# Another order of work in the head of a hybrid decoder layer, earlier loads at the start of its scan, and more buffers for the loads of v

## The chip, the cores and the metric

The kernel runs on one core of a Trainium2 chip. The metric is the device time of one execution in microseconds. Each kernel is run several times, and the median is compared.

## The reference

One layer on 1024 tokens of width 1024, behind 16 learned meta tokens (1040 rows), in float32:

```python
xn = rms_norm(h, mix_pre_g[l])
proj = xn @ w_in[l]                       # z, x, B, C, dt, q, k, v
...
y_ssd = ssd_mixer(z, xbc, dt_raw, ...)    # 2 groups, 16 heads of 64, state 128, chunks of 128
y_sb = rms_norm(stick_breaking_attention(q, k, v).reshape(Bsz, L, SB_WIDTH), sb_norm_g[l])
mix = jnp.concatenate([y_ssd, y_sb], axis=-1) @ w_out[l]
h = h + rms_norm(mix, mix_post_g[l])
xn = rms_norm(h, ffn_pre_g[l])
gu = xn @ w_up[l]
g = causal_dwconv(gu[..., :D_FF], ffn_conv_w[l], ffn_conv_b[l])
f = (jax.nn.gelu(g, approximate=True) * gu[..., D_FF:]) @ w_down[l]
h = h + rms_norm(f, ffn_post_g[l])
```

The mixer convolves x, B and C over four tokens, applies silu, takes dt through a softplus and runs a state space scan by chunks. The attention multiplies q and k of a head, turns the logits z into products of (1 - sigmoid) over the keys between query and key (a running product along the keys), and multiplies the weights with v.

## The kernel before, in words

Five engines work from queues of their own, each in the order of its instructions: TensorE (PE), VectorE (DVE), ScalarE (ACT), GpSimd (POOL), and SyncE (SP), which issues the DMAs. An instruction that waits holds up all that stands behind it on its engine; an instruction order for each engine follows from the order in which the program's text runs, with Python generators that interleave the stages.

A float32 operand of a matmul is split into a high part in a rounded format (fp32r) and a low part, the rest; a product is three matmuls, high by high, high by low, low by high. The high part is a copy on ScalarE, the low part a subtraction on VectorE or GpSimd. Large projections use products of sums of quarters of the operands (t1 to t4 are such sums of x, s24 and others such sums of weights), so that there are fewer products.

**Head** (L325 to L470, L579 to L602). Nine tiles of tokens, the meta tokens first, are loaded (`load_x`, L328), squared and summed by ScalarE (`square`, L354, tile junk), turned into 1/rms by GpSimd (`root`, L361, tiles ms and rs), multiplied by VectorE (`norm`, L365, tile xn) and transposed by TensorE (`turn_x`, L374, tile xtp, eight transposes a tile). A turn is read off by ScalarE (high parts, raw sums) and VectorE (low parts, sums). The weights of B and C of group 0 and of dt come in between (wr_B, wr_C, wr_dt); `split_hi` (L412) and `split_lo` (L418) split them. Their projections are chains of matmuls (`plain_steps`, L208, tiles pj_B and pj_C; `dt_steps`, L242, tile pj_dt): each of four pieces of 260 columns takes 24 matmuls for B and C, which may be cut in two half-chains of 12, and 16 for dt. The pieces go in the order QH: columns 0, then both of the second half of tokens, then 260. ScalarE copies B and C out of PSUM (craw, L236), VectorE dt (tile sq, L249). An explicit sequence at L424 to L463 says when each tile is squared, normed and turned and when a half-chain stands between two turns.

**Duos** (class `Duo`, L258): pairs of 128 columns of the projections of x, z, the other B and C, q and k, seven products each (dA, dX, dY of duo x or z, L308). GpSimd makes the low parts of their weights (wlo, L182) and the sums of weights (L285 to L288), VectorE adds the results (L320). The first duo, d0, begins behind the head. While duos run, the convolutions and transposes of the ones before are done between products.

**v** (L690 to L885). Seven products in the order VORDER, each in two halves s of four tiles t (`v_product`, L801); sums of quarters of the weights are made by `v_sums` (L854; tile vq, L791), and their splits by `v_split` (vwhi L727, vwlo L728). `v_out` stores v on SyncE's queue.

**Scan** (L990 to L1215). Units of a group and a chunk, prepared by `load_bc` (rows sl and sg that build the decay matrix), `load_state` (B, C of the group) and `load_x`; TensorE makes sg (L1059) as the first step of a unit. The projections of the q and k that are left go between the units as fill (`run(fill, n)`, six matmuls each), `put_stores` (L914) issues the stores of the fill that wait.

**Attention** (L1218 to L1480). Eight pairs of heads, eight blocks of queries each. For a block TensorE multiplies k and q (z, L1293), ScalarE takes the sigmoid of it (kp, L1294), VectorE the running product (kp, L1299), TensorE transposes the weights (tw, L1317) and multiplies them with v (av). `load_q` (L961) loads a block's q ahead (four tiles), `load_k` (L952) a pair's k. `load_v` (L1221) loads a pair's v in two versions, v (tile rv, two buffers) and w (tile rw, one buffer, in two pieces of five tiles and four), and GpSimd subtracts the second from the first (L1234). All these loads are issued by SyncE, in the order in which the generators run.

Then come the output projection (mo), the norms, the projections of the feed-forward layer (fA to fY) and the last one (dnA, dnB), where TensorE hardly waits.

## Time and profile before

| | us |
|---|---|
| median of 3 runs | 1688.15 (1682.5 to 1688.64) |
| the profiled execution | 1682.9 |
| its span | 1681.1 |
| TensorE busy in the span | 1635.2 |
| head and first duos | 0 to about 92 |
| v projection | about 350 to 431 |
| start of the scan | 431 to 450 |
| attention | 588 to 870 |

The profile is one execution; its times start at the span's start. Busy times are sums over an engine's instructions. PE is TensorE's matrix work, PEld its loads of weights. A wait names the instruction that waited and the one that ended the wait. The granted clock (PEclk) is the share of full speed that TensorE was given.

### The profile page before, as it was taken

To read this page: it belongs to the slowest core of one execution; us is meant where nothing else is said; L and a number is where in the kernel's file an instruction comes from. 1 tells how busy PE (TensorE), PEld (TensorE's weight loads), DVE (VectorE), ACT (ScalarE), POOL (GpSimd) and SP (SyncE) were. 2 spreads that over 40 slices of the span, in tenths; PEclk is the share of its full clock that TensorE was granted. 3 is DMA by queue.
4 is the path that set the end of the run, shared out by engine and by line. 5 is a ranking of instruction groups with operands and counts; after the bars stand their busy time and mean duration, and the time that the engine had idled before them with its cause. 6 is when DMAs were issued, how large, how long until landed. Compare 5 with 4: busy or idle time off the path is not lost.

```text
span 1681.1 us, 28980 instructions
## 1 busy us (share of the span) xinstructions
PE 1635.2 (97%) x11508; PEld 1442.2 (86%) x11508; DVE 1092.0 (65%) x1250; ACT 746.6 (44%) x1096; POOL 779.8 (46%) x583
## 2 busy tenths in 40 slices
PE   6899999999999999999999999999999999999998
PEld 5899999977877788888877889999998899888886
DVE  7776644345367689988841567666566666658777
ACT  6444344332244367766653245433333333344544
POOL 3576877520366454355332112777777776300001
PEclk9999999999999999999999999999999999999999
DMA  5443335333577875444345542332222333395335
GB/s 189 151 144 116 125 126 183 133 138 140 148 223 238 248 220 177 137 137 124 116 132 172 181 163 94 108 101 94 94 95 95 99 114 101 123 330 183 98 118 178
DMA packets 164518, 247.39 MB, mean 147 GB/s; under 512 B 18487, under 2 KB 99495, under 8 KB 162702
## 3 DMA queue, kind: packets, MB, share of 16 engines
q1 hardware_dynamic: 164382, 245.53, 45.0%
q8 instruction: 91, 1.49, 0.4%
q14 instruction: 45, 0.37, 0.1%
HBM read 161.99 MB, written 83.46 MB: 146 GB/s over the span
## 4 chain that ended last, share of the span: by engine, by line
PE 53%; DMA 0%; POOL 0%; ACT 0%; SPq 0%; issue 0%; DVE 0%; DVEq 0%; POOLq 0%; ACTq 0%
PE fX L1885 10%; PE mo L1489 9%; PE dnA L2297 7%; PE fY L1885 7%; PE fA L1885 7%; PE dnB L2297 5%; PE av L1337 2%; PE tw L1317 1%; PE z L1293 1%; PE g0a L1899 1%; DMA q<-qkd 0%; PE x2tp L1763 0%; PE g0d L1899 0%; PE g0c L1899 0%; PE u0a L1899 0%; PE u0d L1899 0%
## 5 line engine op out<-in xcount | busy, mean ns | idle before, releaser
L1299 DVE TENSOR_TENSOR_SCAN kp<-kp,hold 128x396 f32<-128x396 f32 (+5 forms) x224 | 211.5, 1015 | 30.6 <-ACT kp L1294 28.7
L182 POOL TENSOR_TENSOR wlo<-wr,whi 128x1024 fp32r<-128x1024 f32 x43 | 99.3, 2319 | 41.0 <-ACT whi L181 41.0
L2334 POOL TENSOR_TENSOR fms<-fms 128x1 f32<-128x1 f32 x8 | 2.3, 288 | 222.0 <-DMA ar<-fda 185.9
L181 ACT ACTIVATE whi<-wr 128x1024 fp32r<-128x1024 f32 x43 | 45.7, 1063 | 112.2 <-PE fX L1885 70.8
L1957 DVE SCALAR_TENSOR_TENSOR ga<-gr,pp,ga 128x1024 f32<-128x1024 f32 x44 | 69.3, 1574 | 34.0 <-ACT ga L1950 33.2
L2219 ACT ACTIVATE dh<-ar 128x512 fp32r<-128x512 f32 x77 | 48.6, 631 | 94.5 <-PE dnB L2297 44.7
L1294 ACT ACTIVATE kp<-z 128x788 f32<-128x788 f32 (+4 forms) x96 | 73.0, 833 | 26.5 <-PE z L1293 18.4
L2220 DVE TENSOR_TENSOR dl<-ar,dh 128x512 fp32r<-128x512 f32 x77 | 53.2, 691 | 47.0 <-ACT dh L2219 47.0
L1322 ACT ACTIVATE th<-tw 128x1024 f32<-128x1024 f32 (+2 forms) x96 | 70.8, 813 | 15.5 <-PE tw L1317 15.5
L1293 PE MATMUL z<-k,q 64*128 64x396 f32 (+9 forms) x672 | 65.2, 339 | 10.7 <-DMA q<-qkd 9.7
L1293 PEld LDWEIGHTS z<-k,q 64*128 64x128 f32 x672 | 56.5, 192 | 20.1 <-issue 11.0
L1317 PE MATMUL tw<-ident,kp 128*128 128x128 f32 x576 | 70.0, 276 | 0.8 <-ACT st L926 0.4
L1337 PE MATMUL av<-th,v 128*64 128x128 f32 x1152 | 70.0, 276 | 0.5 <-PE z L1293 0.5
L1317 PEld LDWEIGHTS tw<-ident,kp 128*128 128x128 f32 x576 | 62.4, 141 | 8.0 <-issue 7.2
L2297 PE MATMUL dnA<-dl,dh 128*128 128x512 f32 x176 | 68.5, 389 | 0.0
L2297 PE MATMUL dnA<-dh 128*128 128x512 f32 x176 | 68.5, 389 | 0.0
L2297 PE MATMUL dnA<-dh,dl 128*128 128x512 f32 x176 | 68.5, 389 | 0.0
L1337 PEld LDWEIGHTS av<-th,v 128*64 128x64 f32 x1152 | 62.3, 137 | 6.8 <-issue 4.8
L1271 POOL TENSOR_SCALAR cb<-kp 128x32 f32<-128x32 f32 x64 | 39.9, 632 | 56.4 <-DVE kp L1299 45.2
L2018 POOL TENSOR_TENSOR al<-wr,ah 128x512 fp32r<-128x512 f32 x20 | 28.6, 1428 | 77.6 <-ACT ah L2017 77.5
L2297 PE MATMUL dnB<-dh,dl 128*128 128x512 f32 x132 | 51.4, 389 | 0.0
L2297 PE MATMUL dnB<-dh 128*128 128x512 f32 x132 | 51.4, 389 | 0.0
(987 smaller groups left out, 6042.3 us busy)
## 6 DMA issues: line engine op xcount, KB each, us to landing
wr<-in_w_up SPq DMA_DIRECT2D x44, 512.0 KB
fds<-ga SPq DMA_DIRECT2D x44, 256.0 KB
b<-in_w_down SPq DMA_DIRECT2D x44, 256.0 KB
ar<-fds SPq DMA_DIRECT2D x44, 256.0 KB
fda<-ga SPq DMA_DIRECT2D x33, 256.0 KB
ar<-fda SPq DMA_DIRECT2D x33, 256.0 KB
k<-qkd SPq DMA_DIRECT2D x8, 1040.0 KB
q<-qkd SPq DMA_DIRECT2D x64, 128.0 KB
```

What stands on the lines that cost most here:

```text
L182: nc.gpsimd.tensor_tensor(l, raw, h.bitcast(F32), op=ALU.subtract)
L1293: mm(z[:, j, a - lo:e - lo], u[h, :], r[h, a - bases[x]:e - bases[x]], start=s_ == 0, stop=s_ == 2)
L1294: nc.scalar.activation(kp[:, :, lo:top], z[:, :, :top - lo], AF.Sigmoid, scale=-QSCALE)
L1299: nc.vector.tensor_tensor_scan(part, part, hold[:, L - last + a:L - last + e][:, ::-1], 1.0 if e == last else kp[:, j, e:e + 1], op0=ALU.m ...
L1317: nc.tensor.transpose(tw[:, j, b, :], kp[:, j, c0:c0 + P], ident)
L1322: copied[0] = nc.scalar.activation(th[:, :, :nb, :], tw[:, :, :nb, :], AF.Copy, scale=-1.0, bias=1.0).ins
L1337: mm(av[halves[j], 1 - x, :], v[:, kb, halves[j]], th[:, j, b, :], start=kb == 0, stop=kb == i)
L1489: recent[0] = mm(acc, u[:, k, :], v[:, cs], start=(k == 0 and j == 0), stop=(k == 7 and j == 2))
L1885: mm(acc[:, c, :nn], u[:, k, :], v[:, k, c0:c0 + nn], start=first and k == 0 and j == 0, stop=k == 3 and j == 2, skip_group_check=not first)
L1957: nc.vector.scalar_tensor_tensor(v, self.g[jj][:, :, i:i + 256], fconv_w[:, j, i:i + 1], v, op0=ALU.mult, op1=ALU.add)
L2220: sub(lo[:, k], raw, hi[:, k].bitcast(F32), op=ALU.subtract)
L2297: mm(banks[BANK[n], t], u[:, 0, c], v[:, 1, :], start=(n in (1, 2, 5) and p == 0 and i == 0), stop=(p == NPR - 1 and i == 2), skip_group_c ...
```

## The change

In the head, the load of wr_B goes ahead of gpre (the norm's gain), that of wr_dt gets a buffer of its own and goes behind x3, and that of wr_C goes behind x5. The low parts of B and C are each one subtraction on VectorE instead of two halves on GpSimd. dt is copied out by ScalarE. The pieces of B, C and dt go in the order QC (columns 0 and 260 of the first half of tokens, then of the second), and half-chains or whole chains stand between the turns from the fourth tile on. Behind the head, the splits of the first duo's weights come in another order, and its third split ahead of that of t2.

In the v projection, the tail and the sums of weights for the product behind come one product step earlier, the first split of product 6 too, and the last four stores of v are issued by ScalarE. At the start of the scan, twelve fills stand ahead of the first unit instead of eight, the rows of each of the three buffers are set on their own, and the loads of the second unit are issued behind four fills, ahead of `put_stores`. In the attention, v has three buffers and w two.

```diff
-SCAN_FILL, FIRST = 39, 8
+SCAN_FILL, FIRST = 39, 12
...
-        return raw, plain_steps(w, ev, nm, halves_)
+        return raw, plain_steps(w, ev, nm, halves_, 0, QC)
...
-        for half, c in QH:
+        for half, c in QC:
...
-            nc.vector.tensor_copy(dtT[:, half * TH + c:half * TH + c + CQ], acc[:32, :CQ])
+            nc.scalar.activation(dtT[:, half * TH + c:half * TH + c + CQ], acc[:32, :CQ], AF.Copy)
...
         load_x(0)
         load_x(1)
+        raws = {"B0": raw_of("B0", w_xbc[8])}
         gpre = row_bcast(pre, 0, D, "gpre")
         load_x(2)
         load_x(3)
+        raw_dt = pre.tile([P, KB, 16], F32, tag="wdt", name="wr_dt", bufs=1)
+        nc.sync.dma_start(out=raw_dt, in_=w_dt)
         load_x(4)
-        raw_dt = wp.tile([P, KB, 16], F32, tag="wraw", name="wr_dt")
-        nc.sync.dma_start(out=raw_dt, in_=w_dt)
-        raws = {"B0": raw_of("B0", w_xbc[8])}
-        for i in range(5, NT):
+        load_x(5)
+        raws["C0"] = raw_of("C0", w_xbc[10])
+        for i in range(6, NT + 1):
             load_x(i)
-        raws["C0"] = raw_of("C0", w_xbc[10])
-        load_x(NT)
         nc.sync.dma_start(out=pp, in_=parts)
...
-        def split_lo(name, part):
-            ks = slice(4 * part, 4 * part + 4)
-            nc.gpsimd.tensor_tensor(ws[name][1][:, ks], raws[name][:, ks], ws[name][0][:, ks].bitcast(F32),
-                                    op=ALU.subtract)
-
-        chains = []
-        for i in range(3):
+        def split_lo(name):
+            nc.vector.tensor_tensor(ws[name][1], raws[name], ws[name][0].bitcast(F32), op=ALU.subtract)
+
+        for i in range(2):
             square(i)
             root(i)
         norm(0)
         norm(1)
-        for i in range(NT + 1):
-            if i == 4:
-                run(dt_chain, 1)
-            if i not in (2, 3):
-                norm(i + 2)
-            turn_x(i)
-            if i != 2:
-                square(i + 2 if i == 3 else i + 3)
-                root(i + 2 if i == 3 else i + 3)
-            if i == 3:
-                norm(4)
-                norm(5)
-            if i == 1:
-                hl = tq.tile([P, KB, 32], F32R, tag="wdt", name="wh_dt")
-                nc.scalar.activation(hl[:, :, 0:16], raw_dt, AF.Copy)
-                nc.gpsimd.tensor_tensor(hl[:, :, 16:32], raw_dt, hl[:, :, 0:16].bitcast(F32), op=ALU.subtract)
-                dt_chain = dt_steps(hl)
-            if i in (3, 4):
-                split_hi("B0" if i == 3 else "C0")
-            if i in (3, 4, 5):
-                split_lo("B0" if i < 4 else "C0", int(i == 5))
-            if i == 3:
-                square(6)
-                root(6)
-                split_lo("B0", 1)
-            if i == 3:
-                chains.append(conv_chain("B0", ws["B0"]))
-            if i == 5:
-                raw_x0 = [raw_of(f"x0{j}", w_xbc[j]) for j in range(2)]
-            if i in (5, 6):
-                run(chains[0][1], 1)
-            if i == 6:
-                chains.append(conv_chain("C0", ws["C0"]))
-            if i in (7, 8):
-                run(chains[1][1], 1)
+        split_hi("B0")
+        split_lo("B0")
+        square(2)
+        root(2)
+        norm(2)
+        turn_x(0)
+        square(3)
+        root(3)
+        norm(3)
+        turn_x(1)
+        hl = tq.tile([P, KB, 32], F32R, tag="wdt", name="wh_dt")
+        nc.scalar.activation(hl[:, :, 0:16], raw_dt, AF.Copy)
+        nc.gpsimd.tensor_tensor(hl[:, :, 16:32], raw_dt, hl[:, :, 0:16].bitcast(F32), op=ALU.subtract)
+        dt_chain = dt_steps(hl)
+        chains = [conv_chain("B0", ws["B0"])]
+        square(4)
+        root(4)
+        turn_x(2)
+        norm(4)
+        square(5)
+        root(5)
+        turn_x(3)
+        norm(5)
+        run(dt_chain, 1)
+        split_hi("C0")
+        split_lo("C0")
+        chains.append(conv_chain("C0", ws["C0"]))
+        run(chains[0][1], 1)
+        turn_x(4)
+        square(6)
+        root(6)
+        norm(6)
+        run(chains[0][1], 1)
+        run(chains[1][1], 1)
+        turn_x(5)
+        square(7)
+        root(7)
+        norm(7)
+        run(chains[1][1], 1)
+        run(dt_chain, 1)
+        turn_x(6)
+        square(8)
+        root(8)
+        norm(8)
+        raw_x0 = [raw_of(f"x0{j}", w_xbc[j]) for j in range(2)]
+        run(chains[0][1], 2)
+        turn_x(7)
+        run(chains[1][1], 2)
+        turn_x(8)
...
     d0 = duos[0]
     d0.r = raw_x0
+    d0.split_22()
     run(dt_chain, 1)
-    run(chains[0][1], 2)
-    d0.split_22()
+    run(chains[0][1], 1)
+    d0.split_1()
     split_t(t1r, xo["t1"], nc.vector)
+    run(chains[0][1], 1)
+    d0.sums()
     run(chains[1][1], 2)
     for act in late:
         act()
-    d0.split_1()
-    run(chains[0][1], 2)
-    d0.sums()
     run(dt_chain, 1)
-    run(chains[1][1], 2)
+    d0.split_3()
     xo["t2"] = split_t(t2r, (x_tile(tq, "r1", "t2h"), x_tile(tq, "bh", "t2l")), nc.vector)
-    run(dt_chain, 1)
     run(chains[0][1])
     xo["t3"] = split_t(t3r, (x_tile(tq, "r2", "t3h"), x_tile(tq, "bl", "t3l")), nc.vector)
...
-    d0.split_3()
     run(chains[1][1])
     head.close()
...
-    def v_out(t, half, fh, src):
+    def v_out(t, half, fh, src, eng=nc.sync):
         r0 = half * TH + t * P
-        nc.sync.dma_start(out=vd[r0:r0 + P, 512 * fh:512 * fh + 512], in_=src)
+        eng.dma_start(out=vd[r0:r0 + P, 512 * fh:512 * fh + 512], in_=src)
...
-            v_out(t, 1, 0, vacc[1, t])
+            v_out(t, 1, 0, vacc[1, t], nc.scalar)
...
-                if nx is not None and t == (2 * (1 - s) + s if n == 2 else s):
+                if nx is not None and t == (1 if n == 2 else s):
                     v_split(nx, s)
-                if n == 2 and (s, t) == (0, 3):
-                    v_sums(1)
-                if n == 2 and (s, t) == (0, 1):
+                if n == 2 and (s, t) == (0, 0):
                     v_tail()
                     v_sums(0)
+                if n == 2 and (s, t) == (0, 2):
+                    v_sums(1)
...
-        def load_state(a, b):
-            for g in range(2):
+        def load_state(a, b, gs=range(2)):
+            for g in gs:
...
+            segs.append((sl, sg))
+        pick = sp.tile([32, 8], F32, tag="pick", name="pick")
+        nc.vector.tensor_tensor(pick, ident[:32, 16:24], ident[:32, 24:32], op=ALU.add)
+
+        def set_rows(b):
+            sl, sg = segs[b]
             nc.gpsimd.tensor_copy(sl, ones[:32])
-            if b == 0:
-                pick = sp.tile([32, 8], F32, tag="pick", name="pick")
-                nc.vector.tensor_tensor(pick, ident[:32, 16:24], ident[:32, 24:32], op=ALU.add)
             nc.vector.tensor_scalar(sg, pick.unsqueeze(2).to_broadcast([32, 8, P]), -1.0, None, op0=ALU.mult)
-            segs.append((sl, sg))
 
         def load_bc(g, c):
...
+        set_rows(0)
         load_bc(*units[0])
-        load_state(0, 2)
+        load_state(0, 2, [0])
         nc.sync.dma_start(out=dtk, in_=dtkd)
         load_x(*units[0])
         prev = [None, None]
-        run(fill, 8)
+        run(fill, 4)
+        set_rows(1)
+        load_bc(*units[1])
+        load_state(0, 2, [1])
+        load_x(*units[1])
+        run(fill, FIRST - 4)
         put_stores()
-        load_bc(*units[1])
-        load_x(*units[1])
+        set_rows(2)
         load_bc(*units[2])
         load_zx(*units[0])
-        run(fill, FIRST - 8)
         cur = chunk_weights(*units[0])
         chunk_mask(*units[0], *cur)
-        run(fill, 8)
+        run(fill, 16 - FIRST)
         chunk_decay(*units[0], *cur)
         for n, (g, c) in enumerate(units):
             if n == 12:
...
-        v = rp.tile([P, NT + 1, P], F32, tag="rv", name=f"v{p}")
+        v = rp.tile([P, NT + 1, P], F32, tag="rv", name=f"v{p}", bufs=3)
...
-            w = rp.tile([P, 5, P], F32, tag="rw", name=f"w{p}_{a}", bufs=1)
+            w = rp.tile([P, 5, P], F32, tag="rw", name=f"w{p}_{a}", bufs=2)
...
-        mv = rp.tile([P, NT, P], F32, tag="rv", name="meta_v")[:NM]
+        mv = rp.tile([P, NT, P], F32, tag="rv", name="meta_v", bufs=3)[:NM]
```

Three places in the order of the instructions. TensorE in the head, behind the turn of the fourth tile (pj_dt0 is the first piece of dt, xtp4 and xtp5 are the two halves of the turns of tiles 4 and 5, pj_B0 a piece of B), before:

```order
L247 MATMUL pj_dt_0_0_316<-b11h_131,wh_dt_256 32x260 x4
L247 MATMUL pj_dt_0_0_316<-b21h_133,wh_dt_256 32x260 x4
L247 MATMUL pj_dt_0_0_316<-b11l_132,wh_dt_256 32x260 x4
L247 MATMUL pj_dt_0_0_316<-b21l_134,wh_dt_256 32x260 x4
L383 MATMUL xtp4_0_336<-ident_69,xn4_298 128x128 x4
L383 MATMUL xtp4_1_341<-ident_69,xn4_298 128x128 x4
L383 MATMUL xtp5_0_375<-ident_69,xn5_300 128x128 x4
L383 MATMUL xtp5_1_380<-ident_69,xn5_300 128x128 x4
L218 MATMUL pj_B0_0_0_405<-b11h_131,wh_B0_302 128x260
```

and now:

```order
L247 MATMUL pj_dt_0_0_308<-b11h_131,wh_dt_253 32x260 x4
L247 MATMUL pj_dt_0_0_308<-b21h_133,wh_dt_253 32x260 x4
L247 MATMUL pj_dt_0_0_308<-b11l_132,wh_dt_253 32x260 x4
L247 MATMUL pj_dt_0_0_308<-b21l_134,wh_dt_253 32x260 x4
L218 MATMUL pj_B0_0_0_332<-b11h_131,wh_B0_199 128x260
L218 MATMUL pj_B0_0_0_332<-b11l_132,wh_B0_199 128x260
L218 MATMUL pj_B0_0_0_332<-b11h_131,wl_B0_200 128x260
```

The first half-chain of B stands ahead of the turn of tile 4; before, the turns of tiles 4 and 5 stood between. VectorE at its first norm (xn0 to xn3 are norms of tiles, b11l and b21l low parts of a turned tile), before:

```order
L369 SCALAR_TENSOR_TENSOR xn0_202<-xt0_154,rs_pre0_184,gpre_158 16x1024
L369 SCALAR_TENSOR_TENSOR xn1_204<-xt1_156,rs_pre1_191,gpre_158 128x1024
L369 SCALAR_TENSOR_TENSOR xn2_206<-xt2_160,rs_pre2_198,gpre_158 128x1024
L402 TENSOR_TENSOR b11l_132<-xtp0_0_208,b11h_131 128x4x16
L402 TENSOR_TENSOR b21l_134<-xtp0_1_213,b21h_133 128x4x16
L369 SCALAR_TENSOR_TENSOR xn3_231<-xt3_162,rs_pre3_227,gpre_158 128x1024
L402 TENSOR_TENSOR b11l_132<-xtp1_0_233,b11h_131 128x4x128
L402 TENSOR_TENSOR b21l_134<-xtp1_1_238,b21h_133 128x4x128
```

and now:

```order
L369 SCALAR_TENSOR_TENSOR xn0_195<-xt0_154,rs_pre0_184,gpre_160 16x1024
L369 SCALAR_TENSOR_TENSOR xn1_197<-xt1_156,rs_pre1_191,gpre_160 128x1024
L419 TENSOR_TENSOR wl_B0_200<-wr_B0_158,wh_B0_199 128x1024
L369 SCALAR_TENSOR_TENSOR xn2_210<-xt2_162,rs_pre2_206,gpre_160 128x1024
L402 TENSOR_TENSOR b11l_132<-xtp0_0_212,b11h_131 128x4x16
L402 TENSOR_TENSOR b21l_134<-xtp0_1_217,b21h_133 128x4x16
L369 SCALAR_TENSOR_TENSOR xn3_235<-xt3_164,rs_pre3_231,gpre_160 128x1024
L402 TENSOR_TENSOR b11l_132<-xtp1_0_237,b11h_131 128x4x128
L402 TENSOR_TENSOR b21l_134<-xtp1_1_242,b21h_133 128x4x128
```

The low part of B (wl_B0), which was GpSimd's, stands between the norms of tiles 1 and 2, and the norm of tile 2 behind it. SyncE in the attention, around the loads of the third pair's v (v2, and w2 in two pieces; q2 are its blocks of q), with the semaphores that each waits for, before:

```order
L1224 DMA v2_7045<-vd_3895 128x8x128 [waits DMAHW1_49,PE_49]
L1225 DMA v2_7045<-vcd0_3896 128x128 [waits DMAHW2_49]
L1230 DMA w2_0_7048<-vd_3895 128x5x128 [waits DMAHW3_49,Pool_49]
L1465 DMA yk0_2_7050<-yd2_92 128x1024 [waits DMAHW4_49]
L917 DMA qkd70_548<-st07780_6852 256x1x260 [waits DMAHW5_49,Pool_49]
L917 DMA yd1_99<-ysc0_6540 128x8x128 [waits DMAHW6_49,DVE_49]
L965 DMA q2_7_7098<-qkd20_538 128x2x128 [waits DMAHW7_49]
L965 DMA q2_0_7100<-qkd20_538 128x2x128 [waits DMAHW0_49]
L917 DMA qkd71_549<-st17520_7093 256x1x260 [waits DMAHW1_49,Pool_49]
L1230 DMA w2_5_7169<-vd_3895 128x3x128 [waits DMAHW3_49,DMAHW2_49,Pool_49]
L1232 DMA w2_5_7169<-vcd1_3897 128x128
L965 DMA q2_6_7229<-qkd20_538 128x2x128 [waits DMAHW4_49,PE_49]
```

and now:

```order
L1239 DMA v2_7043<-vd_3893 128x8x128 [waits DMAHW1_49]
L1240 DMA v2_7043<-vcd0_3894 128x128 [waits DMAHW2_49]
L1245 DMA w2_0_7046<-vd_3893 128x5x128 [waits DMAHW3_49,Pool_49]
L1480 DMA yk0_2_7048<-yd2_92 128x1024 [waits DMAHW4_49]
L926 DMA qkd70_616<-st07780_6850 256x1x260 [waits DMAHW5_49,Pool_49]
L926 DMA yd1_99<-ysc0_6538 128x8x128 [waits DMAHW6_49,DVE_49]
L974 DMA q2_7_7096<-qkd20_606 128x2x128 [waits DMAHW7_49,PE_49]
L974 DMA q2_0_7098<-qkd20_606 128x2x128 [waits DMAHW0_49,PE_49]
L926 DMA qkd71_617<-st17520_7091 256x1x260 [waits DMAHW1_49,Pool_49]
L1245 DMA w2_5_7167<-vd_3893 128x3x128 [waits DMAHW2_49]
L1247 DMA w2_5_7167<-vcd1_3895 128x128 [waits DMAHW3_49]
L974 DMA q2_6_7227<-qkd20_606 128x2x128 [waits DMAHW4_49,PE_49]
```

The order is the same; the load of v2 waits no longer for a matmul (PE) and the second piece of w2 no longer for GpSimd (Pool), whereas q2_7 and q2_0 now name a matmul.

## The prediction

> **What bounds the kernel now.** I read the page first (shares by engine, then the chain of work that ended last), then the waits of TensorE, then the timeline at each place where it waits. From the page, the span, TensorE's row and the chain:
>
> ```profile
> span 1681.1 us, 28980 instructions
> PE 1635.2 (97%) x11508; PEld 1442.2 (86%) x11508; DVE 1092.0 (65%) x1250; ACT 746.6 (44%) x1096; POOL 779.8 (46%) x583
> PE 53%; DMA 0%; POOL 0%; ACT 0%; SPq 0%; issue 0%; DVE 0%; DVEq 0%; POOLq 0%; ACTq 0%
> ```
>
> TensorE sets the end: it idles 1681.1 - 1635.2 = 45.9 us, and no other engine has a share of the chain that rounds above nothing. The diff takes no matrix work away, so it can gain only what TensorE waits, and what it runs at a lower clock. The waits (engine, line, releaser: total, times, longest):
>
> ```profile
> PE xtp L383 <- DVE xn L369: 15.0, 6, 8.5
> PE z L1293 <- DMA q<-qkd: 9.7, 6, 2.2
> PE pj_dt L247 <- DVE sq L249: 2.1, 1, 2.1
> PE vB L810 <- DVE vwlo L728: 1.7, 1, 1.7
> PE sg L1059 <- DMA sg<-diagd: 1.5, 1, 1.5
> PE xtp L383 <- ACT junk L359: 1.3, 1, 1.3
> PE sg L1059 <- DMA bt<-bcd: 1.2, 1, 1.2
> PE dYx L308 <- POOL wlo3x L182: 1.0, 1, 1.0
> PE dXx L308 <- DVE craw_x L320: 0.8, 1, 0.8
> PE vB L810 <- ACT vwhi L727: 0.7, 1, 0.7
> PE pj_C L218 <- ACT craw_B L236: 0.5, 1, 0.5
> ```
>
> Four places: the head (rows of xtp, pj_dt, pj_C, dYx, dXx), the v projection (vB), the start of the scan (sg), the attention (z). The change touches all four.
>
> **Head.** TensorE's timeline there (start, duration, what it did, idle before it), and where the first z product begins:
>
> ```profile
> 8.47 1.03 PE L383 MATMUL xtp<-ident,xn 16*128 16x16 f32 x8 [8.47 <-DVE xn L369]
> 20.54 1.07 PE L383 MATMUL xtp<-ident,xn 128*128 128x128 f32 x8 [2.56 <-DVE xn L369]
> 23.58 1.94 PE L383 MATMUL xtp<-ident,xn 128*128 128x128 f32 x8 [1.98 <-DVE xn L369]
> 29.85 0.28 PE L218 MATMUL pj_B<-b21h,wl_B 128*128 128x260 f32 x1
> 29.97 0.28 PE L218 MATMUL pj_B<-b21h,wh_B 128*128 128x260 f32 x1
> 36.62 1.09 PE L383 MATMUL xtp<-ident,xn 128*128 128x128 f32 x8 [1.58 <-DVE xn L369]
> 88.21 0.36 PE L308 MATMUL dAz<-b11h,whi1z 128*128 128x260 f32 x1
> 93.29 0.39 PE L308 MATMUL dXz<-t2h,whi4z 128*128 128x260 f32 x1
> ```
>
> A turn is eight transposes: 1.07 us at full clock, 1.94 at half. A projection matmul follows the one before it after 0.12 us (29.85, 29.97). After the first turn TensorE idles (15.0 - 8.5) + 2.1 + 1.3 + 1.0 + 0.8 + 0.5 = 12.2 us before 88.21. The clock (last columns: granted clock, DMA share, GB/s) and VectorE:
>
> ```profile
> 20.00:30.00 10.00, 7.49 (x40) 7.31 (x41) 7.06 (x12) 6.03 (x17) 5.95 (x8) 0.66 0.19 61
> 90.00:100.00 10.00, 10.00 (x73) 9.80 (x72) 8.78 (x10) 2.57 (x4) 6.06 (x4) 0.83 0.45 160
> 21.16 2.28 DVE L369 SCALAR_TENSOR_TENSOR xn<-xt,rs_pre,gpre 128x1024 f32<-128x1024 f32 x1 [0.77 <-POOL rs_pre L170]
> 35.29 1.27 DVE L369 SCALAR_TENSOR_TENSOR xn<-xt,rs_pre,gpre 128x1024 f32<-128x1024 f32 x1
> 36.48 0.68 DVE L402 TENSOR_TENSOR b12l<-xtp,b12h 128x512 fp32r<-128x512 f32 x1
> ```
>
> Three norms take some 2.3 us instead of 1.27 while GpSimd splits wl_B and wl_C in halves. The change gives VectorE these splits whole, about 1.2 us each (the 128x1024 subtraction at 369.40 below), 2.4 us in all against three times 1.0 us of stretching: about even. It hands four copies of dt to ScalarE, which was busy 6.03 of the 10 us above. What counts is the order: TensorE gets half-chains between turns where it now waits for norms.
>
> Start: wr_B goes ahead of gpre, and the first norms need gpre. 0.52 MB at the 400 GB/s or so of this stretch is 1.3 us:
>
> ```profile
> GB/s 0 0 0 115 115 98 279 401 377 287 262 229 303 434 418 410 418 418 434 391 417 404 401 426 418 426 401 410 401 418 180 8 0 115 254 254 279 418 401 376
> ```
>
> So the first turn moves from 8.47 to about 9.7, and x2 to x5 land as much later, ahead of their norms all the same, which come one every 2 us or slower; wr_C no longer waits on SyncE's queue for GpSimd's split of dt, whose buffer it shared, and x6 to x8 no longer stand behind it. Up to the last turn TensorE then has eight turns, three of them cold (1.0 + 3 x 1.94 + 4 x 1.07 = 11.1 us) and 128 projection matmuls (15.4 us, 0.8 more for the cold ones): 9.7 + 27.3 = 37.0 for the start of the last turn if it never waits. VectorE's own work up to the ninth norm is nine norms (10.8 us at 1.2 from one to the next), two splits (2.4) and the subtractions of turns 0 to 6, 0.6 us each for full tiles (36.48 is the first of a set of five; 11.6 in all): 24.8 us from 8.4 on, done at about 33, so TensorE sets the pace. Before, the last turn began at 36.62 with 52 of these matmuls done. So the last turn comes 0.5 us later with 76 x 0.12 = 9.2 us more work behind it. Of the later waits pj_C's 0.5 and pj_dt's 2.1 go (the copy is ScalarE's now and no longer stands behind t2l); dYx's and dXx's 1.8 may stay. First dAz: 0.5 - 9.2 - 2.6 = -11.3 plus up to 1.5 of longer waits for splits that now come sooner than their inputs: -10 to -11, at about 78.
>
> Then GpSimd is late next. Its z splits run in one chain:
>
> ```profile
> 76.56 2.20 POOL L182 TENSOR_TENSOR wlo1z<-wrz,whi1z 128x1024 fp32r<-128x1024 f32 x1 [2.97 <-ACT whi1z L181]
> 89.54 3.17 POOL L182 TENSOR_TENSOR wlo4z<-s24z,whi4z 128x1024 fp32r<-128x1024 f32 x1
> ```
>
> From 76.56 to 92.71 is 16.15 us, and dXz starts at 93.29, 0.6 behind it. If wlo1z starts about 8.5 us sooner, the chain ends at 84.2, against dXz ready at 82.8: 1.4 to 2.5 us are given back. **Head: -8.5**, between -5.5 (the chain only moves with ScalarE) and -11 (it does not bind).
>
> **v projection.** VectorE's first quarter of the weight sum, alone and beside GpSimd's:
>
> ```profile
> 369.40 1.22 DVE L791 TENSOR_TENSOR vq<-vq,vq 128x1024 f32<-128x1024 f32 x1
> 373.13 3.40 DVE L791 TENSOR_TENSOR vq<-vq,vq 128x1024 f32<-128x1024 f32 x1 [2.51 <-POOL vq L791]
> ```
>
> The change starts these sums one product earlier: six matmuls of 512 columns, 1.4 us by the 0.12 that 260 columns take. Of the 2.4 us of vB's two waits **-1.1** go; from 0 (the parts stretch each other again) to -2.4. The last four v stores go to ScalarE's queue, where nothing but their own additions stands ahead; if not, four issues cost about 2 us there, which the fill hides.
>
> **Scan.** The first sg waits 1.2 and 1.5 us for loads. Twelve fills ahead of it instead of eight put four more, about 2.9 us by the 24 matmuls in them, over the first; the second's loads are issued ahead of the stores of the fill. Both go; GpSimd, which now splits wlo for the fill before its xdt, may cost 0.4. **-2.3**, between -0.5 and -2.7.
>
> **Attention.** SyncE's waits, what it issues after the longest (11.3 us, till GpSimd's v at L1234 has ended), and TensorE:
>
> ```profile
> SPq L1230 <- POOL v L1234: 55.4, 6, 11.3
> 695.14 0.37 SPq L1230 DMA_DIRECT2D w<-vd  x1
> 696.13 1.19 SPq L965 DMA_DIRECT2D q<-qkd  x2
> 698.84 1.51 PE L1293 MATMUL z<-k,q 64*128 64x456 f32 x12 [1.89 <-DMA q<-qkd]
> ```
>
> The second w load has the first one's only buffer to wait for, and the q loads stand behind it; z comes 2.7 us after their issue. Six such waits hold the queue, six times z waits, 9.7 us. With two w tiles and three v tiles the q loads go out some 10 us sooner. Next late would be VectorE, so the question is whether it keeps up:
>
> ```profile
> 600.00:640.00 40.00, 37.99 (x421) 34.43 (x419) 34.48 (x39) 27.00 (x41) 23.71 (x24) 0.96 0.74 236
> 640.00:680.00 40.00, 39.48 (x459) 34.82 (x459) 37.72 (x47) 29.21 (x44) 13.73 (x17) 1.00 0.56 172
> 680.00:720.00 40.00, 38.11 (x414) 33.35 (x413) 35.80 (x40) 29.23 (x42) 17.89 (x17) 1.00 0.52 151
> 760.00:800.00 40.00, 36.50 (x376) 31.90 (x376) 32.12 (x37) 25.79 (x37) 18.83 (x20) 0.96 0.49 143
> ```
>
> In 640 to 680 VectorE is busy 37.7 of 40 us and TensorE idles 0.5. With its 1.9 us gone, 680 to 720 has VectorE at 35.8 of 38.1, the same density. I take 2 of the 9.7 back for it: **-7.7**, from -3 (VectorE takes over in all but the sparse pairs) to -9.7.
>
> **Clock.** The granted clock of 0.96 in 600 to 640 and in 760 to 800 is 1.6 us lost in each; 680 to 720 shows 1.00 with a z wait in it, and 90 to 100 has a dip (0.83) though TensorE is busy 10.00 of 10. The waits may bring the dips or not, so I count half of the two: **-1.6** (0 to -3.2). [...]
>
> **Sum.** -8.5 - 1.1 - 2.3 - 7.7 - 1.6 = -21.2. Against the profiled execution's 1682.9 us (span 1681.1 and 1.8 around it) that is 1661.7. The three runs are 1682.5, 1688.15 and 1688.64: the profiled one lies at the low end, 5.2 under their median, so I add half of that for a median of runs: **1664.3**.
>
> **Rivals.**
> (a) In the attention the queue is merely held elsewhere: q loads wait for z's four q tiles, or VectorE's scans set the pace. For: 37.7 of 40 us. Against: 640 to 680, and five of the z waits directly follow such a w load. Then its 7.7 and the 1.6 of the dips stay away from the sum, and -11.9 is left: 1673.6, with the same 2.6 added as in all that follow.
> (b) The head's lead is lost at the first two duos, where GpSimd's splits, stretched beside VectorE (wlo4z 3.17 against wlo1z's 2.20), bind from the first x products on. For: dYx's wait on wlo3x. Against: it has only ordered work and starts with the weights, which TensorE's order doesn't hold. The head then gives 3.5: 1669.3.
> (c) The change doesn't do what it says: the loads of v still wait (for attention's products, as L1224 does now) and the half-chains find their own inputs late. Only V, scan and half the head are left, -7.7: 1677.8.
> (d) Slower: the clock. The short half-chains between turns leave TensorE at half clock from the first turn to dAx, as in 20 to 30. From about 13 to 53.5 (37.0, the last turn, and 128 more matmuls) lie some 41 us of work; each us done at half clock costs one. All of it: -21.2 + 41 = +19.8, 1705.3. It is slower by more than the bound below from 32 us on. For: 0.66 in one stretch. Against: that followed two gaps of over 1.9 us, at 29.85 the clock was full again, and stayed so over gaps of 1.3 to 2.1.
>
> **Numbers.** Forecast 0.63; (a) 0.14, (b) 0.13, (c) 0.06, (d) 0.04. The terms' ends add up to -9 and -29; they don't all fall together, so about -12 to -26, which with the 0 to 5.7 of the runs' spread, and the other three cases on the faster side taken in, makes 1655 to 1678. About 0.5%, 8.4 us, is what can be told from no change: under 1679.7 counts as faster. Forecast, (a), (b) and a third of (c) lie there, less a rest for their tails: 0.87 faster, 0.10 the same, 0.03 slower.
>
> **What would show it.** Right: the xtp rows keep one wait, of about 9.7 us; last turn at 37 to 38; first dAz near 78; a dXz wait on wlo4z of 1 to 3 us; no sg wait; vB under 1.3; no SyncE wait at the w load and none of z on q. Wrong: a granted clock of 0.8 or less over 10 to 50; z waits on DMA still above 5 us; TensorE's waits on GpSimd's splits above 5 us before 116; or a new wait behind 870, where I expect none.

## The result, and the profile after

The changed kernel takes 1661.66 us (median of 4 runs, 1661.03 to 1663.12) against 1687.22 for the kernel before beside it: ratio 0.9855, interval 0.9834 to 0.9876, so it is faster by about 1.5%, clear of the noise. The forecast was 1664.3, between 1655 and 1678. The profiled execution took 1663.1 us (span 1661.4), 19.8 less than the one before; the sum of the prediction was 21.2. The runs of before scatter by some 6 us and its profiled execution lies at their low end, so the medians differ by more, 25.6.

The page, and the waits of TensorE that replace those shown of before:

```profile
span 1661.4 us, 28993 instructions
PE 1627.9 (98%) x11508; PEld 1433.2 (86%) x11508; DVE 1091.1 (66%) x1248; ACT 747.7 (45%) x1100; POOL 780.6 (47%) x579
```

```profile
PE xtp L383 <- DVE xn L369: 11.6, 5, 9.7
PE st L1120 <- POOL xw L1080: 3.2, 2, 1.9
PE sg L1070 <- DMA sg<-diagd: 1.3, 1, 1.3
PE dYx L308 <- DVE craw_x L320: 1.3, 1, 1.3
PE dXz L308 <- POOL wlo4z L182: 1.0, 1, 1.0
...
PE yt L1136 <- POOL em L1100: 0.9, 1, 0.9
...
PE vB L819 <- DVE vwlo L737: 0.8, 1, 0.8
```

The waits of z for q are gone, and so are those of pj_dt and pj_C in the head. Behind the first turn 1.9 us of waits for norms are left (11.6 - 9.7) where 6.5 stood (15.0 - 8.5); the waits of the first duo stay (dXx 1.3 and dAx 0.7 instead of dYx 1.0 and dXx 0.8). New are two of st for GpSimd and a later one of sg in the scan, and one of dYx at 121. TensorE idles 33.5 us instead of 45.9, and its busy time fell by 7.3 although its 11508 instructions are the same: the clock is the likely part in that, with a mean granted clock of 0.997 instead of 0.991. In the head 20 to 30 now shows 1.00 instead of 0.66:

```profile
20.00:30.00 10.00, 10.00 (x87) 9.79 (x85) 6.90 (x13) 8.38 (x23) 1.36 (x3) 1.00 0.19 55
```

The head on TensorE's timeline, first and last turn and the first products of z:

```profile
9.66 1.03 PE L383 MATMUL xtp<-ident,xn 16*128 16x16 f32 x8 [9.66 <-DVE xn L369]
38.36 1.07 PE L383 MATMUL xtp<-ident,xn 128*128 128x128 f32 x8 [0.27 <-DVE xn L369]
78.35 0.36 PE L308 MATMUL dAz<-b11h,whi1z 128*128 128x260 f32 x1
84.97 0.58 PE L308 MATMUL dXz<-t2h,wlo4z 128*128 128x260 f32 x1 [1.03 <-POOL wlo4z L182]
```

The first turn comes at 9.66 (forecast about 9.7), the last at 38.36 (37 to 38), the first dAz at 78.35 (near 78), and dXz then waits 1.0 us for GpSimd's wlo4z (1 to 3).

Where the time came from is read by stages, from starts on TensorE's timeline (vA is the v projection's first product, which before stands at 345.3 and not at about 350; pj_q is the fill's, mo behind the attention the output projection where it waits 0.97 us for ysc; the last column is the span's end):

| | v starts | fill starts | first z | mo behind the attention | end |
|---|---|---|---|---|---|
| before | 345.3 | 431.5 | 588.1 | 870.0 | 1681.1 |
| after | 338.2 | 422.1 | 580.4 | 850.9 | 1661.4 |
| so far | -7.1 | -9.4 | -7.7 | -19.2 | -19.7 |

So the head gives 7.1 us, v 2.3, the attention 11.5 (281.96 against 270.50 us), what follows 0.5; the stretch of the scan and its fill loses 1.7.

### The profile page after: what moved, and what is told of

It is laid out like the page before. It is cut to its first block, busy times and chain, and to the rows that moved or that the text cites. A ratio compares the mean times of both kernels' runs of the same rounds, so it can differ in the third digit from the quotient of the medians.

```text
span 1661.4 us, 28993 instructions
## 1 busy us (share of the span) xinstructions
PE 1627.9 (98%) x11508; PEld 1433.2 (86%) x11508; DVE 1091.1 (66%) x1248; ACT 747.7 (45%) x1100; POOL 780.6 (47%) x579
## 4 chain that ended last, share of the span: by engine, by line
PE 86%; DVE 4%; DMA 3%; POOL 3%; issue 2%; SPq 1%; ACT 1%; POOLq 0%; DVEq 0%; ACTq 0%
PE fX L1900 10%; PE mo L1504 10%; PE dnA L2312 7%; PE fY L1900 7%; PE fA L1900 7%; PE dnB L2312 5%; PE av L1352 3%; PE tw L1332 3%; PE z L1308 3%; DVE kp L1314 2%; PE dXz L308 2%; PE dXqk L308 2%; PE vA L819 2%; PE pj_q L218 2%; PE pj_k L218 2%
## 5 line engine op out<-in xcount | busy, mean ns | idle before, releaser
L2033 POOL TENSOR_TENSOR al<-wr,ah 128x512 fp32r<-128x512 f32 x20 | 28.6, 1431 | 77.5 <-ACT ah L2032 77.4
L1308 PEld LDWEIGHTS z<-k,q 64*128 64x128 f32 x672 | 53.1, 185 | 10.7 <-ACT th L1337 4.2
```

Of the source, the lines that this page charges most:

```text
L1308: mm(z[:, j, a - lo:e - lo], u[h, :], r[h, a - bases[x]:e - bases[x]], start=s_ == 0, stop=s_ == 2)
```

## The experiments

Each kernel but one is the changed one, with an edit or (once more) without. Their starts at the same places, from the profiled execution of each, and the medians with the ratio to the kernel before on the same chip:

| | median us | ratio, interval | v starts | v | scan | attention |
|---|---|---|---|---|---|---|
| before | | | 345.3 | 86.2 | 156.6 | 282.0 |
| after | 1661.66 | 0.9855 (0.9834 to 0.9876) | 338.2 | 83.9 | 158.3 | 270.5 |
| head of before | 1671.64 | 0.992 (0.9901 to 0.994) | 345.3 | 83.7 | 156.5 | 272.9 |
| scan start of before | 1659.56 | 0.9841 (0.9822 to 0.9859) | 337.1 | 84.3 | 155.6 | 270.4 |
| attention buffers of before | 1671.05 | 0.9915 (0.9897 to 0.9932) | 336.8 | 83.3 | 156.3 | 280.6 |
| v projection of before | 1662.93 | 0.9863 (0.9844 to 0.9882) | 337.0 | 86.1 | 155.5 | 270.5 |
| two v tiles | 1660.15 | 0.985 (0.9822 to 0.9877) | 338.5 | 84.5 | 155.3 | 270.8 |
| one w tile | 1671.07 | 0.9918 (0.9891 to 0.9945) | 337.9 | 84.0 | 157.0 | 281.3 |
| scan's loads first | 1658.26 | 0.984 (0.9812 to 0.9868) | 337.7 | 84.6 | 151.6 | 272.9 |
| gpre first | 1658.28 | 0.9841 (0.9815 to 0.9866) | 336.4 | 83.5 | 154.7 | 271.0 |
| after, once more | 1659.96 | 0.9869 (0.9855 to 0.9882) | 337.3 | 83.3 | 156.7 | 271.0 |
| loads and gpre first | 1655.14 | 0.9836 (0.9823 to 0.985) | 335.4 | 84.0 | 152.3 | 270.5 |
| before with two w tiles | 1672.34 | 0.9944 (0.9931 to 0.9956) | 351.1 | 84.6 | 154.6 | 271.1 |
| low parts by GpSimd | 1660.97 | 0.9874 (0.986 to 0.9887) | 337.6 | 83.3 | 155.6 | 270.5 |

The four kernels behind the changed one were timed beside one another, so were the next four and the last four. Stretches of the same code differ from one profiled execution to the next: the start of v by 1.7 us with the new head (by 5.8 with the old one, in the kernel before with two w tiles), v by 1.3, the scan with the new start by 3.6. The attention without waits for q takes 270.4 to 271.1 us, and 272.9 in two executions; there the granted clock is 0.91 over 600 to 640 in the one and 0.86 over 575 to 600 in the other.

**The head alone undone** (all its edits, the split and the orders behind the turns included):

```diff
-        for half, c in QC:
+        for half, c in QH:
...
-        split_hi("B0")
-        split_lo("B0")
+        for i in range(NT + 1):
+            if i == 4:
+                run(dt_chain, 1)
```

> The changed kernel with the head of before (loads, splits, order of turns and half-chains, copies of dt, first duo's splits). Theory (the places add up, the head is worth what the two traces differ by at the start of the v projection, 338.2 against 345.3): first dAz at 88, v at 345, time 7.1 us above the changed kernel, about 1668.8. Rival (the lead of the head is swallowed later, since the scan waits for loads when TensorE comes early): less than 3 us above it, under 1665.

v starts at 345.3, where the kernel before has it, 7.1 us later than in the changed one. The median is 10 us above it, and 2.4 us of the profiled execution lie in the attention, with its dip of the clock. 20 to 30 is back at a granted clock of 0.66. The lead is not swallowed later: the head's theory stands.

**The scan's start alone undone:**

```diff
-SCAN_FILL, FIRST = 39, 12
+SCAN_FILL, FIRST = 39, 8
...
-        run(fill, 4)
-        set_rows(1)
+        run(fill, 8)
+        put_stores()
         load_bc(*units[1])
-        load_state(0, 2, [1])
         load_x(*units[1])
-        run(fill, FIRST - 4)
-        put_stores()
```

> The changed kernel with the scan start of before (eight fills, loads behind the stores of the fill). From the start of the fill to the first z the changed kernel takes 158.3 us, the one before 156.6. Theory (the early start only moves the wait from sg to the loads of xk two units on, and a clock dip with it): the two sg waits of 1.2 and 1.5 us come back, the st waits on GpSimd's xw go, the stretch takes 156 to 158 and the time is 0 to 2 us below the changed kernel, 1660 to 1662. Rival (the start is worth its 2.6 us, and the later waits come from the lead of TensorE in any case): 2 to 3 us above it, 1664 or more, with the st waits still there.

Its waits in that stretch, then those of the changed kernel there:

```profile
PE yt L1139 <- DVE yt L1114: 1.3, 1, 1.3
PE sg L1068 <- DMA ct<-bcd: 1.2, 1, 1.2
PE sg L1068 <- DMA sg<-diagd: 1.1, 1, 1.1
PE z L1302 <- DVE st L941: 1.0, 1, 1.0
```

```profile
PE st L1120 <- POOL xw L1080: 3.2, 2, 1.9
PE sg L1070 <- DMA sg<-diagd: 1.3, 1, 1.3
PE yt L1136 <- POOL em L1100: 0.9, 1, 0.9
```

The sg waits of the first two units come back, those of st go, and yt waits 1.3 us for VectorE. The stretch takes 155.6 us, and the median is 1659.56: the early start of the scan is worth nothing. The rival's 1664 is ruled out.

**The attention's buffers, together and one by one:**

```diff
-        v = rp.tile([P, NT + 1, P], F32, tag="rv", name=f"v{p}", bufs=3)
+        v = rp.tile([P, NT + 1, P], F32, tag="rv", name=f"v{p}", bufs=2)
...
-            w = rp.tile([P, 5, P], F32, tag="rw", name=f"w{p}_{a}", bufs=2)
+            w = rp.tile([P, 5, P], F32, tag="rw", name=f"w{p}_{a}", bufs=1)
```

> The changed kernel with two v tiles and one w tile again. Theory (the buffers are the whole gain of the attention, 282.0 against 270.5 us from the first z to the last): the waits of z for q come back, six of 1 to 2 us, and 11.5 us with the dips of the clock behind them, about 1673. Rival (the dips have nothing to do with the waits): 8 to 9 us, about 1670, granted clock 1.00 in all stretches of the attention.

> The changed kernel with two v tiles again, w still with two. Theory (the wait that held the q loads was that of the second w load for GpSimd's subtraction from the first): SyncE's waits for av at the load of v come back (some 40 us), but z does not wait for q; within 1 us of the changed kernel. Rival (v's buffer is needed too, since the load of v stands ahead of two q loads): z waits 3 us or more, 3 to 6 us slower.

> The changed kernel with one w tile again, v still with three. Theory (it is w's buffer): the waits of SyncE at the second w load for GpSimd are back, z waits for q six times or nearly so, 9 to 11.5 us slower, about 1672. Rival (the third v tile lets GpSimd subtract earlier, so w comes free in time): under 4 us slower.

TensorE's and SyncE's waits in the attention. With both undone:

```profile
PE z L1308 <- DMA q<-qkd: 8.8, 6, 2.1
```

With two v tiles and two w tiles (SyncE, then TensorE, where no row names q):

```profile
SPq L1239 <- PE av L1375: 40.0, 6, 8.9
```

```profile
PE z L1308 <- DVE st L941: 1.0, 1, 1.0
PE mo L1504 <- DVE ysc L1381: 1.0, 1, 1.0
PE av L1352 <- DVE thc L1367: 0.6, 2, 0.3
```

With three v tiles and one w tile:

```profile
SPq L1245 <- POOL v L1249: 66.4, 6, 13.4
```

```profile
PE z L1308 <- DMA q<-qkd: 8.1, 5, 2.1
```

With both undone the attention takes 280.6 us, 10.1 more, and the median is 9.4 us above the changed one, between what the theory and the rival gave. SyncE stands 40.0 us at the load of v when v has two tiles, and it costs nothing: no z waits for q, 270.8 us. It stands 66.4 us at the load of w when w has one, and 281.3 us are back. These are two waits of the same queue, and only one of them holds q loads till they are late; in the order shown, a q load stands right behind the second w load, while others stand between the load of v and the next q. The theory of w holds in both directions; the third v tile does nothing here.

**The kernel before with two w tiles**, its only edit:

```diff
-            w = rp.tile([P, 5, P], F32, tag="rw", name=f"w{p}_{a}", bufs=1)
+            w = rp.tile([P, 5, P], F32, tag="rw", name=f"w{p}_{a}", bufs=2)
```

> The kernel before with one edit: two w tiles instead of one. Theory (this buffer alone holds the q loads, whatever the rest does): no z wait for q, the attention takes 270.5 to 271 us instead of 282, about 11 us below the kernel before, ratio 0.9935, near 1675. Rival (the third v tile or the earlier fill takes part): 4 to 8 us below, some of the z waits left.

The attention takes 271.1 us, 10.9 less, and no z waits for q; the ratio is 0.9944, interval 0.9931 to 0.9956, which holds the theory's 0.9935. The rest of that execution lost 5.8 us ahead of v (351.1), 3.05 of them in one wait of dYx, on which more below.

**The v projection alone undone:**

```diff
-                if n == 2 and (s, t) == (0, 0):
+                if n == 2 and (s, t) == (0, 3):
+                    v_sums(1)
+                if n == 2 and (s, t) == (0, 1):
                     v_tail()
                     v_sums(0)
-                if n == 2 and (s, t) == (0, 2):
-                    v_sums(1)
```

> The changed kernel with the v projection of before (sums one product later, last stores from SyncE). Theory: both waits of vB come back (0.7 and 1.7 us) and the stretch of the v projection takes 86.2 us instead of 83.9: 2.3 us above the changed kernel, about 1664, half of it the dip of the clock. Rival (the waits depend on where the dip of the clock falls, not on the order): within 1 us of the changed kernel.

Both waits are back, 0.7 and 1.7 us, and the stretch takes 86.1 us:

```profile
PE vB L819 <- DVE vwlo L737: 1.7, 1, 1.7
PE vB L819 <- ACT vwhi L736: 0.7, 1, 0.7
```

The granted clock of 0.94 over 360 to 390 is back with them, as in the kernel before. The kernel before with two w tiles has the same two waits, a clock of 1.00 there, and 84.6 us. So the dip does not belong to the waits. The waits add up to 1.6 us less with the new order (2.4 against 0.8), but without the dip the old order is only 0.7 us slower (84.6 against 83.9), with 1.3 us of scatter: how the 2.3 divide between order and dip is not settled. The whole time cannot tell 2 us: 1662.93 lies inside the scatter.

**The scan's loads first:**

```diff
+            if n + 2 < len(units):
+                load_x(*units[n + 2])
+            if n + 3 < len(units):
+                load_bc(*units[n + 3])
             if n < 2:
                 put_stores()
...
-            if n + 3 < len(units):
-                load_bc(*units[n + 3])
-            if n + 2 < len(units):
-                load_x(*units[n + 2])
```

> The changed kernel, and in each unit of the scan the loads of xk (two units on) and of sl and sg (three units on) issued first, ahead of the stores of the fill, the loads of B and C, of z and of x. Theory (the new waits of the scan, sg 1.3, st 1.4 and 1.9, and the dip at 470, come from these loads standing behind others on SyncE's queue): they go, and the time is 3 to 5 us below the changed kernel, about 1657.5. Rival (the transfers are late because the DMA engines are full, 0.65 to 0.9 busy there): the waits move to zk, xd or the state's loads, and the time is within 1.5 us of it.

GpSimd's work on the first and the third full unit in the changed kernel, with the wait for xk, and when SyncE issued xk for them:

```profile
450.66 1.04 POOL L1075 TENSOR_TENSOR xdt<-xk,dtk 128x512 f32<-128x512 f32 x1 [5.06 <-DMA xk<-xsd]
...
468.04 1.04 POOL L1075 TENSOR_TENSOR xdt<-xk,dtk 128x512 f32<-128x512 f32 x1 [5.53 <-DMA xk<-xsd]
```

```profile
447.87 0.35 SPq L1048 DMA_DIRECT2D xk<-xsd  x1
...
462.92 0.35 SPq L1048 DMA_DIRECT2D xk<-xsd  x1
```

And with the loads first:

```profile
445.72 1.04 POOL L1075 TENSOR_TENSOR xdt<-xk,dtk 128x512 f32<-128x512 f32 x1
452.11 1.04 POOL L1075 TENSOR_TENSOR xdt<-xk,dtk 128x512 f32<-128x512 f32 x1 [0.71 <-DMA xk<-xsd]
460.18 1.04 POOL L1075 TENSOR_TENSOR xdt<-xk,dtk 128x512 f32<-128x512 f32 x1 [3.62 <-DMA xk<-xsd]
```

```profile
441.40 0.34 SPq L1048 DMA_DIRECT2D xk<-xsd  x1
...
454.81 0.37 SPq L1048 DMA_DIRECT2D xk<-xsd  x1
```

In the changed kernel xdt starts 2.8 us after the issue of its load in the first unit and 5.1 us in the third; GpSimd idles 5 us for it, and st waits for xw right behind. With the loads first the first is issued 6.5 us sooner and xdt starts 5 us sooner, no sg or st wait is left, and the stretch takes 151.6 us. In place of those waits stands one of yt for VectorE's xd, 1.0 us, as the rival had it, but not of their size. So the place on the queue made these loads late. That full DMA engines add to it is not ruled out: the third unit's xdt still starts 5.4 us after the issue (454.81 to 460.18), and GpSimd idles 3.6 us for it, but TensorE no longer waits there. The median, 1658.26, is where the theory put it, though its interval overlaps that of the changed kernel.

**gpre first:**

```diff
-        raws = {"B0": raw_of("B0", w_xbc[8])}
         gpre = row_bcast(pre, 0, D, "gpre")
+        raws = {"B0": raw_of("B0", w_xbc[8])}
```

> The changed kernel with gpre ahead of wr_B again. Theory (TensorE sets the pace of the head from the fourth turn on, so a start 1.2 us sooner is kept until GpSimd's z splits): first turn at 8.4, first dAz 0.5 to 1.2 us sooner, dXz waits for wlo4z 1 us more, and the time is 0 to 1 us below the changed kernel. Rival (wr_B's later landing delays ScalarE's and VectorE's splits ahead of the second and third norm, so the third and fourth turns come no sooner): no gain at dAz, or up to 1 us slower.

The first turn is at 8.5 and the first dAz at 76.9 instead of 78.4, v starts at 336.4. Both executions with gpre first have dAz at 76.9 and 77.0, the eight with wr_B first and the low parts on VectorE at 77.4 to 79.5. So the place of wr_B ahead of gpre costs about 1.5 us at the head; the theory had 0.5 to 1.2. The median, 1658.28, is below that of the changed kernel in both of its comparisons, but the intervals of the ratios overlap.

**Once more, and both orders of loads together:**

> The changed kernel once more, unaltered, beside the three that follow on the same chip. Expected within 2 us of its first median, 1661.7. It tells which of the stretches differ from execution to execution: the dYx wait of 1.3 us at 121 and the second st wait at 470 stood in some of the kernels with the same code there and not in others. Theory (they depend on which of VectorE and GpSimd comes first): one of them or both are gone in this execution. Rival (they belong to the code): both are there.

> The changed kernel with gpre ahead of wr_B and the scan's loads of xk, sl and sg first in each unit. Theory (the two act in different places, and what the scan gains is passed on): about 4 to 6 us below the changed kernel beside it, 1656, no sg or st wait of over 0.5 us. Rival (the lead of the scan is taken back at the start of the attention, where the one with the loads first took 272.9 us against 270.5): 2 to 3 us below, 1658.5.

The unaltered kernel took 1659.96 us; the dYx wait of 121 was not there, the second st wait 0.4 instead of 1.9. With both orders of loads the median is 1655.14, the ratio 0.9836 (0.9823 to 0.985) against 0.9869 (0.9855 to 0.9882) beside it: faster than both kernels by more than the intervals. v starts at 335.4, the scan takes 152.3 and the attention 270.5, so its lead is not taken back.

**The low parts of B and C by GpSimd, at the same places:**

```diff
         def split_lo(name):
-            nc.vector.tensor_tensor(ws[name][1], raws[name], ws[name][0].bitcast(F32), op=ALU.subtract)
+            nc.gpsimd.tensor_tensor(ws[name][1], raws[name], ws[name][0].bitcast(F32), op=ALU.subtract)
```

> The changed kernel with the low parts of B and C made by GpSimd again, each in one subtraction, at the same places of the text. Theory (the order of the half-chains is the gain, who makes the low parts is about even): first dAz within 1 us of 78.4, time within 1.5 us of the changed kernel. Rival (the splits on VectorE are what keeps the norms short and GpSimd free for the roots): the norms beside them take 2.3 to 3.5 us again, the roots stand behind a split of 2.2 us, first dAz 2 to 4 us later, time 2 to 4 us above it.

The first dAz is at 79.2, 0.8 us later, with a wait of 1.7 us of pj_C for wl_C, and the median 1660.97. The norms from the third tile on take 1.28 us each, so the rival's stretched norms are not there. Who makes the low parts is about even at these places, as the prediction had it. The gain of the head lies in its other edits; of these only the place of gpre was tried alone, and the order of the half-chains was not parted from the loads and the copy of dt.

## Why the prediction was right, and the term that was not

**What bounds it.** That no other engine has a share was read off a chain that accounts for 53% of the span. Of the changed kernel it accounts for nearly all: 86% TensorE, 4% VectorE, 3% each DMA and GpSimd. The idle time, 45.9 us before and 33.5 now, bears out that TensorE sets the end.

**Head, -8.5 forecast, -7.1 measured** (-6.8 to -8.5 in the other kernels with this head). The sum up to the first dAz came out: 9.66, 38.36, 78.35, and GpSimd's chain gave back 1.0 of it. (76 times 0.12 is 9.1, not 9.2; the forecast of about 78 does not hang on it.) The rest went at 121.34, in a wait that the forecast did not have. VectorE and GpSimd there, in the changed kernel and in the kernel before:

```profile
118.50 2.18 DVE L664 TENSOR_TENSOR s<-s 128x144 f32<-128x144 f32 x1
120.60 0.69 DVE L320 TENSOR_TENSOR craw_x<-dYx,craw_x 128x520 f32<-128x520 f32 x1
```

```profile
118.33 2.19 POOL L182 TENSOR_TENSOR wlo3z<-wrz,whi3z 128x1024 fp32r<-128x1024 f32 x1
```

```profile
126.71 0.31 DVE L655 TENSOR_TENSOR s<-s 128x144 f32<-128x144 f32 x1
126.94 0.69 DVE L320 TENSOR_TENSOR craw_x<-dYx,craw_x 128x520 f32<-128x520 f32 x1
```

```profile
126.98 2.20 POOL L182 TENSOR_TENSOR wlo3z<-wrz,whi3z 128x1024 fp32r<-128x1024 f32 x1 [0.46 <-ACT whi3z L181]
```

A multiplication on VectorE (s by itself, a step of dt's softplus) that took 0.31 us in the kernel before, where GpSimd's split of 2.2 us began 0.27 us behind it (126.98 against 126.71), took 2.18 in the changed one, where the split began 0.17 us ahead of it (118.33 against 118.50), and dYx waited for the addition behind it. The execution of the changed kernel once more, with the same code, had VectorE ahead by 0.7 us and no such wait. In all 14 profiled executions it took 2.17 to 2.19 us in the three where the split began first, by 0.17 to 0.24 us, and 0.31 in the eleven where it began later. In the changed kernel it ended at 120.68, 0.16 us behind the end of the split, and in the other two of the three 0.17 us behind it; why it took as long as that is not shown.

**v, -1.1 forecast, -2.3 measured:** in its range; 0.7 to 1.6 us are the order's, the rest the clock's dip or scatter.

**Scan's start, -2.3 forecast, +1.7 measured: the step that failed.** The prediction said of the two sg waits "Both go", and of GpSimd that it "may cost 0.4". These two went. But the loads of the units behind stand where they stood on SyncE's queue, behind the stores of the fill and the loads of B, C, z and x, and TensorE now comes to them sooner: sg 1.3, st 1.4 and 1.9 us. I had not asked what is next late there; the front of the queue was checked, not the row behind it. The kernel with the old start takes as long (155.6), the two with the loads first 151.6 and 152.3, 2.3 us or more below every other with the new start. That the stretch is worse by 1.7 in this pair and not by 0 is within what executions differ by (154.7 to 158.3 with the new start).

**Attention, -7.7 forecast, -11.5 measured with the clock,** for which 1.6 more were set down. The mechanism was as told, and only w's buffer was needed. The 2 us kept back for VectorE were not needed: it is denser than before and TensorE is not held.

```profile
640.00:680.00 40.00, 40.00 (x454) 34.97 (x454) 38.99 (x46) 32.18 (x45) 13.75 (x18) 1.00 0.67 198
680.00:720.00 40.00, 39.56 (x436) 34.57 (x434) 37.47 (x39) 28.75 (x42) 25.77 (x22) 1.00 0.38 111
760.00:800.00 40.00, 39.69 (x428) 34.51 (x425) 35.61 (x41) 27.75 (x40) 18.24 (x17) 1.00 0.50 144
```

VectorE is busy 38.99 of 40 us and TensorE 40.00. So the rival that VectorE takes over is ruled out, and so is the one that q's four tiles hold the loads till z waits: SyncE waits 19.9 us for z at the q loads now (18 times, at most 4.0), and no z waits for them.

**Clock, -1.6 forecast.** Both dips of the attention are gone in this pair. But with the waits back (both buffers undone) the one at 760 to 800 is not, and four kernels without any wait of z for q have a dip at the attention's start (0.86 to 0.93 over 575 to 600). That the waits bring the dips is therefore not shown; what does stays open. The rival of a head at half clock is ruled out: the granted clock, 0.50 over 23.5 to 25.6 in the kernel before, is 1.00 in each 10 us from 20 to 80, and projection matmuls follow one another after 0.12 us from 20.83 on.

**The median.** Half of 5.2 us was added for the runs' place above the profiled execution. The changed kernel's profiled execution, 1663.12, was the slowest of its four runs and lies 1.5 above their median, so here that addition was 4.1 too much; the sum promised 1.4 us too much (21.2 against 19.8), and the two errors partly cancel. That the sum itself came so near is in part luck: the scan's 4.0 us and the head's 1.4 that did not come were made up for by 2.2 more in attention and clock, 1.2 more in v and 0.5 behind the attention.

## What to carry to other kernels

When a wait of the bound engine is taken away, follow its queue one row further: in the scan the next load on the same queue was late by as much as the first had been, and moving the loads to the front of each unit shortened the stretch, which the earlier start had not. When several loads stand on one in-order queue, ask which of its waits has a load that is due right behind it; 40 us of waiting at one place cost nothing and 66 at another cost 11. Time a part alone before it is kept: of four parts here two carried 18 of the 20 us, one was worth nothing, and one buffer of two was idle.

## What the runs showed of the hardware

- A VectorE multiplication that took 0.31 us in eleven executions took 2.17 to 2.19 in the three where GpSimd's split of 2.2 us had begun 0.17 to 0.24 us ahead of it, and ended 0.16 to 0.17 us behind the split. Which comes first changed between executions of the same kernel, and TensorE's wait behind it was 0, 1.3, 1.5 (with two v tiles) or 3.05 us (in the kernel before with two w tiles).
- The first turn stood at 9.5 to 11.0 us in the nine profiled executions with wr_B ahead of gpre, and at 8.4 to 8.6 in the five with gpre ahead of wr_B: the uncertainty of 1 us or more goes with the load ahead of gpre.
- The granted clock fell in single windows at places without a wait (0.91 over 80 to 100 in the kernel before, TensorE busy 20.00 of 20 us), and at others only in some executions (over 575 to 600, 1.00 in the changed kernel and 0.93 in the same kernel once more).
- At the start the granted clock and the durations disagree: over 10 to 20 us of the changed kernel the clock reads 1.00, while a turn of a full tile takes 1.97 us there and 1.03 to 1.07 from 22 us on.

```profile
10.86 1.97 PE L383 MATMUL xtp<-ident,xn 128*128 128x128 f32 x8 [0.16 <-DVE xn L369]
22.27 1.04 PE L383 MATMUL xtp<-ident,xn 128*128 128x128 f32 x8
```
